# Feed-forward chunks with weights stationary, four-kilobyte expert loads, and rooms held later in a joined kernel

## The chip, the cores and the metric

The kernel runs on one core of one Trainium2 chip. The metric is the device time of one execution in microseconds (us). TensorE (PE) multiplies a stationary 128 x 128 block by moving columns into banks of PSUM; VectorE (DVE), ScalarE (ACT) and GpSimd (POOL) work on vectors; SyncE (SP) issues most DMA loads from HBM into SBUF. Each engine takes its own instructions in program order.

## What is computed

x has 256 tokens of 1024 features, everything in float32. Two layers of a first block are followed by two layers of a second block. Cut to what matters here:

```python
def swiglu(x, w_gate, w_up, w_down):
    return (silu(x @ w_gate) * (x @ w_up)) @ w_down

def first_block(x, ...):
    for l in range(2):
        x = x + 0.5 * swiglu(rms_norm(x, ffn1_norm[l]), ...)   # 1024 -> 2816 -> 1024
        h = rms_norm(x, mix_norm[l])
        ...                                                    # three attentions, gated and merged
        x = x + merged @ w_out[l]
        x = x + 0.5 * swiglu(rms_norm(x, ffn2_norm[l]), ...)

def second_block(x, mem, ...):
    for l in range(2):
        ...                                                    # linear attention and spatial gating
        x = layer_norm(DN_ALPHA * x + h, ...)
        h = mem_xattn(x, mem, wq[l], wk[l], wv[l], wo[l])      # keys: mem @ wk[l], 256 memory rows
        x = layer_norm(DN_ALPHA * x + h, ...)
        h = grouped_moe(x, ...)                                # 16 experts, 1024 -> 512 -> 1024, 2 per token
        x = layer_norm(DN_ALPHA * x + h, ...)
```

In `grouped_moe`, each expert computes `silu(x @ w_gate[e]) * (x @ w_up[e]) @ w_down[e]`, and its rows are added with the token's gate weight.

## The kernel before

**Stages.** TensorE goes through four feed-forward blocks (FFN) with the mixing stages between them, then for each layer of the second block: linear attention and gating, attention to the memory, sixteen experts. The keys of the memory for layer 1 are made right after the experts of layer 0, since the weights lie in the same stream.

**The weight stream.** All large weights come in units of 512 KB (128 partitions x 1024 floats) in the order of use. SBUF is cut into "rooms" of one unit. `load_ahead` (L262 to L274) puts the next unit into a free room; its DMA is issued by SP at L272. `take`/`hold` set rooms aside for other data, `give` returns them. Eight DMA semaphores go round over all DMA issues, so an issue waits until the eighth before it has landed, whichever engine issued that. PE, ACT, DVE and POOL take instructions in the order in which the program is written; `tick` lets queued side work (`spawn`, generators) go on between products.

**Products in float32.** `mm3` makes one product out of three fast ones: a weight is split into a rounded part (`whi`, ACT, L310) and its rest (`wlo`, DVE, L284), and so is the other factor. `pump` (L276) does the splitting ahead of use. Expert weights are marked `whole`: they are used unsplit with plain float32 products, and `pump` stops at any open whole unit when it runs ahead.

**FFN** (`gated`, L515 to L626). The 2816 hidden columns go in chunks, `CUTS` (L46): 512, 256 and four times 512. Of each chunk `into` makes the gate and then the up product, with x transposed (`xt`) stationary and the weights as moving columns, for two halves h of 128 tokens. ACT takes silu of the gate; DVE multiplies by the up product (L609). The result has tokens on its partitions and must be transposed before it can be the stationary factor of the down product: `turned` (L552) does up to four transposes (L558), an ACT copy (L561) and a DVE subtraction (L562). These stand after the second unit of the next chunk's gate. `down` adds to four banks `ys`. `last_down` ends each (half h, column half j), whose result DVE adds to x (L633), and transposes of the new x (L432) follow.

**Experts** (`moe`, L1700 to L2022). Each expert gets up to 64 token places. `gather(q)` collects the rows of x for four experts by products with a 0/1 matrix `pick` (L1834), the results copied by DVE (L1840) or ACT (L1842) into `xg`. `into(e)` (L1925) makes gate and up for the expert in one bank, in four steps u; `turn(e)` transposes (L1939), takes silu and multiplies (L1942); `down(e)` (L1950) makes the down product, scaled into two parts (L1956, L1957); `way_back(e)` makes the transposed 0/1 matrix and gate weights (L1851 on POOL, L1856, L1859, L1860); `scatter(e)` (L1966) adds the expert's rows to `ys`. The loop over e is at L1987 to L2018. In it `turn(e)` comes in step 0 of `into(e+1)` and `scatter(e-1)` in step 2; the gathers for experts 4 to 15 are spawned at e = 1, 4 and 8. Transposes and gathers share the banks "tp", products the banks "mm": three of "mm" and one of "tp" (L1975).

**Memory** (`memory`, L1341 to L1356, and `turned`, L1358 to L1377). In layer 0, `ME` = 9, 12, 20 sets the experts: from e = 9 eight rooms are set aside, at e = 12 the memory rows are loaded into `stage` (L1347, issued by ACT), and after 20 ticks they are transposed (L1354, copies at L440). `turned` multiplies the key weights, stationary, with the transposed memory of 256 columns (L1371 to L1373).

Of the kernel before, what the change touches and what calls it, by code (L numbers as in the profile page):

```python
# [42 lines left out]
ME = 9, 12, 20  # L43
P0 = (0,), (0,)
FN = 9, 9, 2, 4
CUTS = [512, 256, 512, 512, 512, 512]  # L46
# [23 lines left out]
def the_kernel(  # L70
# [90 lines left out]
    def columns(c0, n, pool, *loads):  # L161
# [5 lines left out]
        def put():  # L167
            pt = bank("mm")[:, :n]
            nc.tensor.transpose(pt, rows, ident[:n, :n])
            nc.vector.tensor_copy(col[:, c0:c0 + n], pt)  # L170
# [93 lines left out]
    def load_ahead(upto=None):  # L264
# [3 lines left out]
        while len(loads) < min(len(units), upto or len(units)) and free:  # L268
            at = free.pop(0)
            w, c0, n, k0, m, _, _ = units[len(loads)]  # L270
            r = block(at, [UNIT], name="raw")[:, :m * n].rearrange("p (k n) -> p k n", n=n)
            nc.sync.dma_start(r, w[k0 * P:(k0 + m) * P, c0:c0 + n].rearrange("(k p) n -> p k n", p=P))  # L272
# [3 lines left out]
    def pump(most=1, hurry=False, upto=None):  # L276
# [12 lines left out]
        while len(parts) < len(units) and (most > 0 if upto is None else len(parts) <= upto):  # L289
# [7 lines left out]
            if upto is None and any(whole is True for *_, whole in units[now["closed"]:len(parts)]):  # L297
                break
# [216 lines left out]
    def gated(xt, ready, chunks, scale, factor, last=True, renew=None, between={}, up="tp"):  # L515
# [3 lines left out]
        ys = []  # L519

        def into(tag, halves, hooks, done):
            W = Taken()
            o = [bank(tag)[:, :W.n] for _ in range(NH)]
            if halves == "start":

# [13 lines left out]
            order = [(h, u) for h in range(NH) for u in range(W.count)] if halves else \  # L539
                [(h, u) for u in range(W.count) for h in range(NH)]  # L540
            for i, (h, u) in enumerate(order):
                for k in W.ks(u):
                    mm3(o[h], *xt.at(h, k), *W(k), k == 0, k == KD - 1)
                if h:
                    W.close(1)
                if u == W.count - 1:
                    done(h, o[h])
                tick()
                for at, f in hooks:
                    if at == i + 1:  # L550
                        f()

        def turned(h, u, n):

            tp = tbank()
            nf = n // P
            for f in range(nf):
                nc.tensor.transpose(tp[:, f], u[:, f * P:(f + 1) * P], ident)  # L558
            uh = t2(FR).rearrange("p (f t) -> p f t", t=P)
            ul = t2(FR).rearrange("p (f t) -> p f t", t=P)  # L560
            nc.scalar.activation(uh[:, :nf], tp[:, :nf], AF.Copy)  # L561
            nc.vector.tensor_sub(ul[:, :nf], tp[:, :nf], uh[:, :nf].bitcast(FT))  # L562
            return uh, ul

        def down(c, ut):
            W = Taken()
            if not ys:
                ys.extend([bank(ACC[h]) for _ in range(2)] for h in range(NH))
            for f in range(W.kt):
                for h in range(NH):  # L570
                    for j in range(2):
                        mm3(ys[h][j], *(t[:, f] for t in ut[h]), *W(f, j), c == 0 and f == 0, False)
# [4 lines left out]
        def last_down(c, ut, gs):  # L577
            W = Taken()
            if not ys:
                ys.extend([bank(ACC[h]) for _ in range(2)] for h in range(NH))  # L580
            for h in range(NH):
                for j in range(2):
                    for f in range(W.kt):
                        mm3(ys[h][j], *(t[:, f] for t in ut[h]), *W(f, j), c == 0 and f == 0, last and f == W.kt - 1)
                        if (h, j) == (1, 1):
                            W.close(1)
                        if h == j == 0 and f == 1:
                            ut[1] = turned(1, late[1], late[2])
                        if f == W.kt - 1 and renew:
                            gs[h].append(spawn(renew(h, j, ys[h][j])))  # L590
                        if f % 2:
                            tick()
# [46 lines left out]
    def mixing_constants(fb, tmp):  # L639
# [52 lines left out]
        def distances():  # L692

            for put in puts:
                put()
# [1415 lines left out]
```

## Time and profile before

| | |
|---|---|
| three runs, median (lowest to highest) | 2193.13 us (2188.81 to 2196.97) |
| the profiled execution | 2191.49 us |
| its span in the profile | 2189.8 us |
| TensorE busy | 97% of the span, 11117 instructions |
| VectorE, ScalarE, GpSimd busy | 51%, 41%, 8% |
| moved by DMA | 490.48 MB, mean 224 GB/s |

The page of the profile gives the busy time of each engine over the whole span. A view of windows gives the same for stretches, with TensorE's granted clock (PEclk, 1.00 is full speed), the busy share of the DMA engines and the rate. A view of waits gives what an engine stood idle for. A timeline lists an engine's instructions in order, like neighbours put together.

### The profile page before, as it was taken

The numbers are of one execution on the slowest core, as the hardware profiler recorded it, in microseconds if no ns is written. First come the engines' busy times: TensorE is split into PE (matmuls) and PEld (weight loads), VectorE is DVE, ScalarE is ACT, GpSimd is POOL, SyncE is SP. The second block draws the span as 40 slices with busy tenths as digits, with TensorE's granted clock in tenths as the row PEclk, the third lists the DMA queues.
The fourth block names the chain that finished last, engine by engine and source line by source line (L and its number), as shares of the span: only waits on it lengthen the run. The fifth ranks groups of instructions, "written<-read, shape, count | busy, mean of one in ns | idle before, by whom it ended". The sixth has DMA issues, their size and how long they took to land. (4 is left out here: it accounts for less than half of the span.)

```text
span 2189.8 us, 29392 instructions
## 1 busy us (share of the span) xinstructions
PE 2117.0 (97%) x11117; PEld 1554.0 (71%) x11117; DVE 1118.9 (51%) x1999; ACT 892.4 (41%) x1424; POOL 172.5 (8%) x231
## 2 busy tenths in 40 slices
PE   8999999999999999999999999989999999989997
PEld 6778878788888888787888887963333677953332
DVE  6445787554555547866554547651111558341112
ACT  5444555454444446554544454521111454421111
POOL 1000100100000002102000002011000111010000
PEclk9999999999999999999999999999999999999999
DMA  7554643556556655535756555679998936589996
GB/s 250 187 181 149 211 145 111 178 177 200 174 172 193 196 159 171 187 98 173 242 183 190 158 170 198 207 258 338 393 394 297 360 116 236 178 313 383 394 393 247
DMA packets 240076, 490.48 MB, mean 224 GB/s; under 512 B 17539, under 2 KB 44851, under 8 KB 239923
## 3 DMA queue, kind: packets, MB, share of 16 engines
q1 hardware_dynamic: 239634, 487.42, 65.9%
q8 instruction: 92, 1.51, 0.3%
q10 hardware_dynamic: 288, 1.05, 0.1%
q14 instruction: 62, 0.50, 0.1%
HBM read 487.34 MB, written 1.07 MB: 223 GB/s over the span
## 5 line engine op out<-in xcount | busy, mean ns | idle before, releaser
L284 DVE TENSOR_TENSOR wlo<-raw,whi 128x1024 fp32r<-128x1024 f32 (+1 forms) x508 | 614.7, 1228 | 292.7 <-ACT whi L310 288.3
L310 ACT ACTIVATE whi<-raw 128x1024 fp32r<-128x1024 f32 (+1 forms) x508 | 525.1, 1052 | 293.3 <-PE tp L359 115.7
L1925 PE MATMUL mm<-raw,xg 128*64 128x512 f32 x1024 | 243.7, 604 | 7.7 <-PEq L1981 7.0
L357 PE MATMUL accB<-whi,xt 128*128 128x512 f32 (+3 forms) x448 | 176.2, 393 | 0.0
L359 PE MATMUL accB<-whi,xt 128*128 128x512 f32 (+3 forms) x448 | 165.5, 369 | 0.0
L358 PE MATMUL accB<-wlo,xt 128*128 128x512 f32 (+3 forms) x448 | 165.3, 369 | 0.0
L1925 PEld LDWEIGHTS mm<-raw,xg 128*64 128x64 f32 x1024 | 69.8, 137 | 133.5 <-issue 123.0
L357 PE MATMUL tp<-whi,xt 128*128 128x512 f32 (+1 forms) x384 | 143.8, 374 | 0.0
L359 PE MATMUL tp<-whi,xt 128*128 128x512 f32 (+1 forms) x384 | 143.4, 373 | 0.0
L358 PE MATMUL tp<-wlo,xt 128*128 128x512 f32 (+1 forms) x384 | 142.5, 371 | 0.0
L357 PE MATMUL mm<-whi,xt 128*128 128x512 f32 (+1 forms) x320 | 121.2, 379 | 1.4 <-DVE nbias L715 0.7
L359 PE MATMUL mm<-whi,xt 128*128 128x512 f32 (+1 forms) x320 | 118.3, 370 | 0.0
L358 PE MATMUL mm<-wlo,xt 128*128 128x512 f32 (+1 forms) x320 | 117.6, 368 | 0.0
L1950 PE MATMUL mm<-raw,t 128*64 128x512 f32 x512 | 117.3, 599 | 0.0
L1930 ACT ACTIVATE t<-mm 128x512 f32<-128x512 f32 x32 | 19.1, 597 | 188.4 <-PE mm L1925 188.4
L359 PEld LDWEIGHTS accB<-whi,xt 128*128 128x128 f32 x448 | 84.1, 188 | 15.1
L357 PEld LDWEIGHTS accB<-whi,xt 128*128 128x128 f32 x448 | 84.5, 189 | 13.3 <-issue 1.0
L358 PEld LDWEIGHTS accB<-wlo,xt 128*128 128x128 f32 x448 | 84.5, 189 | 11.6
L1859 DVE TENSOR_SCALAR back<-tp 128x256 fp32r<-128x256 f32 x32 | 13.6, 425 | 149.2 <-PE tp L1856 149.2
L609 DVE SCALAR_TENSOR_TENSOR t<-tp,ss,t 128x512 f32<-128x512 f32 (+1 forms) x48 | 33.8, 704 | 104.9 <-PE tp L359 104.9
L359 PEld LDWEIGHTS tp<-whi,xt 128*128 128x128 f32 x384 | 72.1, 188 | 13.5
L358 PEld LDWEIGHTS tp<-wlo,xt 128*128 128x128 f32 x384 | 72.1, 188 | 13.4
(515 smaller groups left out, 3950.2 us busy)
## 6 DMA issues: line engine op xcount, KB each, us to landing
raw<-in_w_gate_dram SPq DMA_DIRECT2D x128, 512.0 KB
raw<-in_w_up_dram SPq DMA_DIRECT2D x128, 512.0 KB
raw<-in_w_down_dram SPq DMA_DIRECT2D x128, 512.0 KB
raw<-in_w_in_dram SPq DMA_DIRECT2D x120, 512.0 KB
raw<-in_ffn_w_gate_dram SPq DMA_DIRECT2D x88, 512.0 KB
raw<-in_ffn_w_up_dram SPq DMA_DIRECT2D x88, 512.0 KB
raw<-in_ffn_w_down_dram SPq DMA_DIRECT2D x88, 512.0 KB
raw<-in_w_out_dram SPq DMA_DIRECT2D x32, 512.0 KB
```

What stands on the lines that cost most here:

```text
L284: eng.tensor_sub(lo, r, hi.bitcast(FT))
L310: nc.scalar.activation(hi, r, AF.Copy)
L357: nc.tensor.matmul(o, xh, wh, start=first, stop=False)
L358: nc.tensor.matmul(o, xh, wl, start=False, stop=False)
L359: nc.tensor.matmul(o, xl, wh, start=False, stop=last)
L609: nc.vector.scalar_tensor_tensor(ss[h], o, factor(h), ss[h], op0=OP.mult, op1=OP.mult)
L1859: nc.vector.tensor_scalar(bk, tp, 0.0, None, op0=OP.is_gt)
L1925: nc.tensor.matmul(p[half(i)], xgs[e // 4][k // 4][:, k % 4, e % 4], W.whole(k, i), start=k == 0, stop=k == KD - 1)
L1930: nc.scalar.activation(c[e], p, AF.Copy)
L1950: nc.tensor.matmul(p[half(j)], uu[e][:, f], W.whole(f)[:, j * 512:(j + 1) * 512], start=f == 0, stop=f == 3)
```

## The change

Four parts.

1. **FFN.** The first chunk stays at 512 columns; the other 2304 go in nine chunks of 256. For these, `into_turned` takes a 128 x 128 block of the weight as the stationary factor and the 256 tokens of `xt` as moving columns, so that the result lies transposed already. Its normalisation factor now lies along the free axis: at chunk 1 two small products and a copy make `roots`, and DVE multiplies the gate by it ahead of silu. Each product is split into its parts without a transpose; only the first chunk's goes through `turned`. The last chunk's up product is made one block of 128 after the other. `last_down` takes a new order. The side work in `between` moves behind the gate and from the "mm" to the "tp" banks, in one step more.
2. **Expert weights.** Gate and up units are loaded so that partition p holds adjacent rows: two rows, 4 KB, in one piece, where before it was pieces of 2 KB. The copies of x for the gathers are permuted to match (`eighths`).
3. **The order of the experts.** Two banks "mm" and two "tp". `turn(e)`, `way_back(e+1)`, `scatter(e-1)` and one quarter of the next gather all stand in step 1 of `into(e+1)`. POOL's part of the way back is issued ahead of `into`. The rooms of `xg` are taken at the start and kept until e = 15, and the memory attention sets aside 6 rooms instead of 4.
4. **Memory of layer 1.** `ME` = 12, 13, 14: the eight rooms are set aside from e = 12, the memory rows loaded at e = 13, and transposed after 14 ticks. `pump` may split later units while up to four whole units are open: the key weights while the last expert's down products run.

```diff
-ME = 9, 12, 20
+ME = 12, 13, 14
-CUTS = [512, 256, 512, 512, 512, 512]
+CUTS = [512] + 9 * [256]
@@ load_ahead
-            nc.sync.dma_start(r, w[k0 * P:(k0 + m) * P, c0:c0 + n].rearrange("(k p) n -> p k n", p=P))
+            if whole is True and m > 1:
+                nc.sync.dma_start(r, w[:, c0:c0 + n].rearrange("(p k) n -> p k n", p=P)[:, k0:k0 + m])
+            else:
+                nc.sync.dma_start(r, w[k0 * P:(k0 + m) * P, c0:c0 + n].rearrange("(k p) n -> p k n", p=P))
@@ pump
-            if upto is None and any(whole is True for *_, whole in units[now["closed"]:len(parts)]):
+            if upto is None and sum(whole is True for *_, whole in units[now["closed"]:len(parts)]) > 4:
                 break
@@ gated
+        ys = [[bank(ACC[h]) for _ in range(2)] for h in range(NH)]
...
+        def into_turned(tag, done, hook=None, in_turn=False):
+            W = Taken()
+            o = [bank(tag)[:, :S] for _ in range(2)]
+            for fs in ((0,), (1,)) if in_turn else ((0, 1),):
+                for u in range(W.count):
+                    for k in W.ks(u):
+                        xh, xl = xt.both(k)
+                        for f in fs:
+                            wh, wl = (t[:, f * P:(f + 1) * P] for t in W(k))
+                            mm3(o[f], wh, wl, xh, xl, k == 0, k == KD - 1)
+                            if k == KD - 1:
+                                done(f, o[f])
+                        if (k + 1) % (4 // len(fs)) == 0:
+                            tick()
+                    if 1 in fs:
+                        W.close(1)
+                    if hook and u == 0:
+                        hook()
+        def parts(u, to):
+            nc.scalar.activation(to[0], u, AF.Copy)
+            nc.vector.tensor_sub(to[1], u, to[0].bitcast(FT))
+            return to
...
+        def last_down(ut):
+            W = Taken()
+            gs = [[], []]
+            for i, (h, j, f) in enumerate(((0, 0, 0), (0, 1, 0), (1, 0, 0), (0, 0, 1), (0, 1, 1), (1, 0, 1), (1, 1, 0),
+                                           (1, 1, 1))):
+                mm3(ys[h][j], *at(ut, h, f), *W(f, j), False, f == 1)
+                if f:
+                    gs[h].append(spawn(renew(h, j, ys[h][j])))
+                if i % 2:
+                    tick()
+            W.close()
+            return gs
...
+            if c == 1:
+                p = bank("tp")[:, :S]
+                for h in range(NH):
+                    nc.tensor.matmul(p[:, h * P:(h + 1) * P], rs[h][:, 0:1].to_broadcast([P, P]), ident, start=True,
+                                     stop=True)
+                roots.append(pool.tile([P, S], FT, name="roots"))
+                nc.vector.tensor_copy(roots[0], p)
+            def silu_turned(f, o):
+                if f == 0:
+                    silus[0] = t2()
+                nc.vector.tensor_mul(silus[0][:, f * S:(f + 1) * S], o, roots[0])
+                if f:
+                    nc.scalar.activation(silus[0], silus[0], AF.Silu)
+            def product_turned(f, o):
+                v = silus[0][:, f * S:(f + 1) * S]
+                nc.vector.tensor_mul(v, o, v)
+                if f == 0:
+                    silus[1:] = [t2(FR), t2(FR)]
+                if c < chunks - 1 and f:
+                    parts(silus[0], silus[1:])
+                elif c == chunks - 1:
+                    parts(v, [t[:, f * S:(f + 1) * S] for t in silus[1:]])
...
+            into_turned("mm", silu_turned, hook)
             if c in between:
                 between[c]()
+            down(c - 1, (True, before) if c == 1 else ut)
+            into_turned("tp", product_turned, in_turn=c == chunks - 1)
+            ut = False, silus[1:]
@@ moe
-        xg_rooms, xn_rooms = [], take(4, 4)
+        xg_rooms, xn_rooms = take(2, 2), take(4, 4)
+            eighths = lambda t, j: t.rearrange("p (k m) -> p k m", k=KD)[:, :, j * 64:j * 64 + 64]
-                    nc.scalar.activation(xn[0][h][:, j * 512:(j + 1) * 512], x[h][j], AF.Copy)
+                    nc.scalar.activation(eighths(xn[0][h], j), x[h][j].rearrange("p (m k) -> p k m", k=KD), AF.Copy)
...
-            turns.enter_context(banks(mm=3, tp=1))
+            turns.enter_context(banks(mm=2, tp=2))
...
-                if e in (1, 4, 8):
-                    gs.append(spawn(gather(len(gs))))
+                if e in (3, 7):
+                    rest_of = gather(e // 4 + 2)
+                    next(rest_of)
...
-                wt = spawn(way_back(e + 1))
-                into(e + 1, {0: lambda: turn(e), 2: lambda: e and scatter(e - 1)})
-                finish(wt)
+                pk = gated_places(e + 1)
+                def between():
+                    turn(e)
+                    way_back(e + 1, pk)
+                    if e:
+                        scatter(e - 1)
+                    next(rest_of, None)
+                into(e + 1, {1: between})
                 down(e, (lambda: turn(15)) if e == 14 else None)
```

## Rows read from the trace of the kernel before

**Rows 1.** The page, busy time of each engine: us, share, instructions.

```profile
PE 2117.0 (97%) x11117; PEld 1554.0 (71%) x11117; DVE 1118.9 (51%) x1999; ACT 892.4 (41%) x1424; POOL 172.5 (8%) x231
```

**Rows 2.** Windows in one FFN: window, us, engines' busy us, PEclk, DMA, GB/s.

```profile
656.75:823.15 166.40, 166.00 (x802) 138.54 (x800) 84.26 (x93) 73.82 (x94) 0.79 (x2) 1.00 0.57 181
674.16:679.81 5.65, 5.65 (x49) 5.65 (x48) 1.21 (x2) 2.12 (x2) 0.00 (x0) 1.00 0.39 116
696.76:707.74 10.98, 10.98 (x49) 9.01 (x48) 3.62 (x4) 4.24 (x4) 0.00 (x0) 1.00 0.60 205
741.60:753.48 11.88, 11.88 (x58) 9.84 (x57) 7.28 (x8) 4.85 (x6) 0.00 (x0) 1.00 0.65 203
...
811.48:814.87 3.39, 2.99 (x16) 2.15 (x13) 2.77 (x4) 0.60 (x1) 0.00 (x0) 1.00 0.88 279
```

**Rows 3.** Windows in layer 0's experts: without a gather, with, and several.

```profile
1586.23:1599.08 12.85, 12.85 (x65) 4.48 (x63) 1.93 (x4) 1.67 (x3) 1.19 (x2) 1.00 1.04 395
1599.08:1618.37 19.29, 17.67 (x96) 8.39 (x94) 3.98 (x8) 2.86 (x5) 1.19 (x2) 1.00 1.04 392
1534.00:1645.00 111.00, 107.76 (x542) 42.29 (x542) 18.54 (x40) 15.06 (x27) 8.72 (x15) 1.00 1.04 394
```

**Rows 4.** Window at the end of layer 0's experts.

```profile
1645.75:1665.00 19.25, 19.25 (x96) 6.75 (x94) 3.11 (x6) 2.74 (x5) 1.21 (x3) 1.00 0.45 160
```

**Rows 5.** Timeline of PE, 1668 to 1684: start, us, instruction, idle before.

```profile
1670.11 3.65 PE L1950 MATMUL mm<-raw,t 128*64 128x512 f32 x16
1673.95 1.07 PE L1925 MATMUL mm<-raw,xg 128*64 128x512 f32 x2 [0.18 <-DMA raw<-in_w_gate_dram]
...
1677.16 0.66 PE L1939 MATMUL tp<-ident,t 128*128 128x128 f32 x4
```

**Rows 6.** Waits of PE, 1670 to 1730: us in total, times, longest.

```profile
PE mm L1373 <- DVE wlo L284: 4.6, 3, 2.6
PE tp L1856 <- DVE mem L440: 1.5, 1, 1.5
PE tp L1354 <- DVE mem L440: 1.4, 1, 1.4
PE tp L1354 <- DVE gw L1860: 0.9, 1, 0.9
```

**Rows 7.** Windows in the key products, weights stationary, 256 columns.

```profile
1251.40:1271.30 19.90, 19.90 (x178) 19.90 (x177) 11.73 (x12) 10.26 (x16) 0.00 (x0) 1.00 0.86 270
...
1737.50:1740.20 2.70, 2.70 (x25) 2.70 (x24) 2.44 (x4) 2.09 (x3) 0.00 (x0) 1.00 1.09 334
```

**Rows 8.** Waits of PE, 1477 to 1670.

```profile
PE tp L1834 <- DVE t L1942: 2.9, 3, 1.1
PE tp L1834 <- ACT xg L1842: 2.1, 3, 0.7
PE tp L1856 <- DVE t L1942: 1.1, 1, 1.1
```

**Rows 9.** Timeline of DVE, 198 to 205.

```profile
199.16 0.75 DVE L609 SCALAR_TENSOR_TENSOR t<-tp,ss,t 128x512 f32<-128x512 f32 x1 [0.31 <-PE tp L359]
...
201.61 0.69 DVE L562 TENSOR_TENSOR t<-tp,t 128x512 fp32r<-128x512 f32 x1 [0.56 <-ACT t L561]
```

**Rows 10.** Timeline of SP's queue, 1568 to 1584: issues of the loads.

```profile
1569.71 0.38 SPq L272 DMA_DIRECT2D raw<-in_w_up_dram  x1
1571.07 0.37 SPq L272 DMA_DIRECT2D raw<-in_w_gate_dram  x1
...
1574.98 0.38 SPq L272 DMA_DIRECT2D raw<-in_w_up_dram  x1
1576.26 0.37 SPq L272 DMA_DIRECT2D raw<-in_w_gate_dram  x1
```

**Rows 11.** Timeline of SP's queue, 2148 to 2176: the last weight loads.

```profile
2148.59 7.08 SPq L272 DMA_DIRECT2D raw<-in_w_down_dram  x6
```

**Rows 12.** Waits of SP's queue, 1640 to 1670.

```profile
SPq L272 <- DMA stage<-in_mem_dram: 19.5, 2, 19.2
```

More of the change, by code (lines that the diff above doesn't have):

```diff
@@ L512, in first_norm, with gated, into @@
         return xt, rs
-    def gated(xt, ready, chunks, scale, factor, last=True, renew=None, between={}, up="tp"):
-        ys = []
-        def into(tag, halves, hooks, done):
+    def gated(pool, xt, ready, chunks, rs, renew, between):
+        ys = [[bank(ACC[h]) for _ in range(2)] for h in range(NH)]
+        def into(tag, done, ordered):
             W = Taken()
             o = [bank(tag)[:, :W.n] for _ in range(NH)]
-            if halves == "start":
+            if ordered:
                 for i, parts in enumerate(((0, 0), (0, 1), (1, 0))):
@@ L538, in into @@
                 return
[L539 to L563, printed above, removed]
+            for u in range(W.count):
+                for h in range(NH):
+                    for k in W.ks(u):
+                        mm3(o[h], *xt.at(h, k), *W(k), k == 0, k == KD - 1)
+                    if h:
+                        W.close(1)
+                    if u == W.count - 1:
+                        done(h, o[h])
+                    tick()
@@ L571, in down @@
                     for j in range(2):
-                        mm3(ys[h][j], *(t[:, f] for t in ut[h]), *W(f, j), c == 0 and f == 0, False)
+                        mm3(ys[h][j], *at(ut, h, f), *W(f, j), c == 0 and f == 0, False)
                     if h:
@@ L575, in down @@
                     tick()
-        def last_down(c, ut, gs):
+        def last_down(ut):
             W = Taken()
[L579 to L592, printed above, removed]
@@ L692, in distances @@
         def distances():
-            for put in puts:
-                put()
-            pv = bank("mm")[:12, :384]
+            pv = bank("tp")[:12, :384]
             nc.tensor.matmul(pv, ct[:, 384:396], ct[:, :384], start=True, stop=True)
@@ L704, in distances, with positions @@
             nc.vector.tensor_scalar(nsink, nsink, -1.0, None, op0=OP.mult)
-            pp = bank("mm")
+        def positions():
+            for put in puts:
+                put()
+            pp = bank("tp")
             nc.tensor.transpose(pp[:, :32], pr, ident[:32, :32])
@@ L1852, in way_back @@
                                             gates[:, h, e:e + 1], None, op0=OP.mult)
-                yield from wait(WB)
+                return pk
+            def way_back(e, pk):
                 tp = tbank()[:, :2]
@@ L2064, in the_kernel @@
             memT = new_memory(4)
-            parts = memory(memT[0], "mm", 2)
+            parts = memory(memT[0], "tp", 2)
             step = lambda: next(parts, None)
```

103 lines of the change are left out of this document (49 added, 54 removed).

## The prediction

> **What bounds the kernel now.** I read the busy shares first: TensorE is busy for 97% of the span, every other engine for 51% or less [rows 1]. So time comes from three places only: columns that TensorE streams, the pitch at which it streams them, and its few waits. Then I took stretches. In a feed-forward block (FFN) TensorE works through 166.00 of 166.40 us at a granted clock of 1.00, which is the 2.4 GHz level, and DMA is at 0.57 [rows 2]: matmul work alone sets that time. In the expert stretches TensorE is almost as full, but DMA stands at 1.04 and 394 GB/s [rows 3]: the loads run slower than the products and live on a lead built up earlier. At the end of layer 0's experts that lead breaks: for 19.25 us the core moves only 160 GB/s [rows 4], and waits follow [rows 5, 6]. The waits views name who was late.
>
> **FFN, four of them.** Before, 48 matmuls of 512 columns take 10.98 us (228.8 ns each) and 48 of 256 columns 5.65 us (117.7 ns) [rows 2]. The gate and up products of the chunks after the first are 384 of the one and 96 of the other: 87.9 + 11.3 = 99.2 us per FFN. After, the same columns are 18 blocks of 128 x 8 x 2 x 3 = 864 matmuls of 256 columns with the weight stationary. The trace has that very form in the key products: 113 ns in the best stretch (19.90 us, 178 records, two of them not matmuls of this kind), and 25 in 2.70 us, with 119.9 ns between neighbours, in the worst [rows 7]. I take 116 ns, between them and near the FFN's own 117.7: 100.2 us, +1.0 (97.9 to 103.6). The weight loads of this form are as long as the stretch in the row, so the array has little slack behind them.
> Halving the moving columns is what the Trainium skill advises against ("TensorE: Matmul & The Clock Gate", sections Back-to-back issue gap and Why this matters for your kernels: 512 columns 518 cycles, 256 columns 262, keep dimensions at 512 or more). By its table two halves cost 1.2% more than a whole, some 1.1 us per FFN; the rows, 2 x 113.3 against 228.8 at best and 2 x 119.9 at worst, reach from a small gain to 5%. The row decides.
> The results now lie transposed, so 36 of 44 transposes per FFN go. Eight of them lengthen 48 matmuls from 10.98 to 11.88 us [rows 2], 0.9 per eight: -4.0. The transpose just ahead of the last down products makes that stretch 3.39 with 2.99 busy, where twelve matmuls want 2.75 [rows 2]: -0.65. Added are two small fp32 matmuls and a copy for the roots; I price them as one round trip through a bank, 0.9, like the mean of the three 2.9 us of waits for a bank in [rows 8], with 0.2 (the matmuls alone) as the low end. Added on DVE are two multiplications per gate block; DVE has 84.26 of 166.40 busy [rows 2] and I expect some 58%. The cover that decides: from a product to its two split parts the old kernel needs 199.16 to 202.30, 3.1 us, with another split between [rows 9]; the next chunk's gate, 48 x 0.116 = 5.6 us, runs meanwhile. Without that cover each chunk would cost the difference, 2 to 3 us. The last down product is put in a new order in which all four quarters finish in its last 3.5 us, so the next stage's renewal follows more tightly: I take +0.9 (0.3 to 2).
> Sum: +1.0 - 4.0 - 0.65 + 0.9 + 0.9 = **-1.9 per FFN, -8 for four** (by the pitch alone -17 to +6). Loads of the narrower chunks come in 1-KB rows, but DMA at 0.57 and 181 GB/s [rows 2] has room; nothing is late there.
>
> **Experts, both layers.** An expert without a gather takes 12.85 us, one with it 19.29 with 17.67 busy [rows 3]. The gathers, turns and way-backs share one transpose bank and wait on its readers: 2.9 + 2.1 + 1.1 = 6.1 us in layer 0 [rows 8], and the same three numbers in layer 1. With two banks, and one quarter of a gather per expert, each bank's reader has a turn of the other bank to finish: **-6.1**. The four hooks become one per expert, so TensorE changes less often between matmul kinds; no row prices a change alone, the excess of a gather expert over a plain one after waits and its 4 x 1.13 us of products is under 0.4 per gather, and I estimate **-1.5** (0 to -2). The product bank count falls from 3 to 2: a gate-up result is copied by ACT while the down product fills the other; the first gather alone uses these two and may wait 0 to 1 us. POOL's selection is issued one expert-part earlier; POOL is idle for 92% [rows 1]. Strided copies of x for the permuted rows: 0 to +3 per layer, taken at 0 since ACT and DVE are far from full. Layer 1: **-7.6** (-10 to -4).
> *Packets.* Gate and up weights go from 2-KB to 4-KB pieces, which down weights already have. SP issues a unit when the one eight before has landed; the pace is 1.36 us for units that follow gate and up loads and 1.28 for those that follow down loads [rows 10]. An expert's twelve units take 12 x 524.288 KB / 394 GB/s = 15.97 us [rows 3]; all at 1.28 it is 15.36. TensorE needs (16 x 12.85 + 3 x 6.44)/16 = 14.06 now and 13.58 after. So over 16 experts the loads lose 30.6 us now and 28.5 after: the lead, which has some 8 us over at the end of layer 1 (the last unit is issued by 2155.7 and lands about 10 later, the span having 24 left) [rows 11], holds.
> Two sections of the Trainium skill ("DMA: Bandwidth & Descriptors") pull against this term: Where 436 GB/s comes from sets about 358 GB/s as the HBM limit, by which packet size would change nothing, as in rival B below; the trace's 394 GB/s contradicts that. Why small descriptors are slow gives a fixed few cycles per descriptor, by which I estimate 2% rather than the rows' 5.5%; the row decides.
>
> **End of layer 0.** SP stands 19.2 us on the loads of the memory rows, which ACT issues only at its place in expert 12 [rows 12]; nothing is loaded meanwhile [rows 4]. Afterwards eight products take from 1673.95 to 1677.16, 3.21 us, where sixteen had just taken 3.65 [rows 5]: 1.4 lost, and with two like stretches beside it some 3.0 us. The memory transposes wait on the single bank 1.5 + 1.4 + 0.9 = 3.8 us, and the key products wait 4.6 us on split weights [rows 6]. After, the memory step is queued one expert later (what waits behind its two loads is again SP's whole weight queue, through the shared semaphores), two banks take the 3.8, the shorter stop and faster units the 3.0. The key weights come earlier by about 16 x 0.6 + 2 = 12 us while TensorE comes earlier by 14, so that the new right to split them under the last four down units gets something to split, but not everything: I take half of 4.6, 2.3 (0 to 4.6). Layer 0: -6.1 - 1.5 - 3.8 - 3.0 - 2.3 = **-16.7** (-22 to -8).
>
> **Sum.** -8 - 7.6 - 16.7 = -32.3 from the profiled execution's 2191.5 (span 2189.8): 2159.2. That execution lies 1.6 below the median 2193.1 of the runs shown, so 2161 as a median.
>
> **The rivals.**
> *E, better pitch:* all 864 matmuls at 113.3 ns: 864 x 2.7 ns x 4 = 9.3 less, **2152**. For it speaks the long key stretch, which had splits on ACT and DVE beside it [rows 7]; against it that the FFN's own 256-column products stay at 117.7 [rows 2].
> *C, worse pitch:* 119.9 ns: 864 x 3.9 ns x 4 = +13.5, **2174**. For it speaks that weight loads fill the whole stretch [rows 7], so each small hitch counts; the stretch of the worst row had DMA and splits beside it as an FFN has.
> *B, the loads don't quicken:* descriptors stay as short in effect, or reads of a 16-KB pitch lose what longer pieces gain. Then 38.2 us of lead are wanted where 38.6 are there, and the 3.0 and 2.3 at the end of layer 0 stay, for the early split has nothing to split: +5.3, **2166**; two waits at the layers' ends could make it 2172.
> *D, slower than before:* each partition now owns eight adjacent weight rows (16 KB), and a gate or up unit reads two of them, so its 4-KB pieces lie 16 KB apart. If that slows a unit beyond 1.36 us, each further 0.1 us costs 12.8 us per layer. At 330 GB/s, 1.59 us, an expert loads in 17.84; (17.84 - 13.58) x 16 - 38.6 = 29.6 per layer, **2220**. Down loads, whole rows in order, say nothing of it; no row here reads at that pitch in that order. [...]
>
> **How the numbers follow.** Forecast A 0.45, E 0.15, B 0.15, C 0.17, D 0.08. The range takes in E, B and C with a margin of their unknown ends (roots, renewal, strided copies): 2146 to 2184; outside are D and about 0.1 of tails. About 0.5%, 11 us, is what a measurement here can tell from no change. Faster: 0.42 of A, E, 0.11 of B, 0.10 of C, 0.78 in all; the same 0.03 + 0.04 + 0.07 = 0.14; slower 0.08.
>
> **What would show it.** Right: FFN of 164 to 165 us with 256-column pitches near 116 ns; no transposes but eight in an FFN's middle; no tp wait in the expert stretches; SP's pace 1.28 throughout; no DMA wait in experts 13 to 15; split of key weights seen before the last down product ends. Wrong: an FFN over 170 us or waits of its down products on split parts (the chain is longer than 5.6 us); a gate unit above 1.36 us; TensorE waiting on raw weights in the middle of a layer.

## The result

The changed kernel takes 2156.1 us (2154.5 to 2156.4) where the kernel before, run beside it, takes 2191.0: a ratio of 0.9835 (0.9813 to 0.9858), some 35 us less. Forecast were 2161 and a range of 2146 to 2184. The profiled execution spans 2154.7 us, 35.1 less than that of before. Where the 35.1 us lie, by the starts of stages in the two traces (first product of the stage on TensorE; one execution each; differences taken before rounding):

| stage | before | after | difference | forecast |
|---|---|---|---|---|
| start to the memory keys of layer 0 (four FFNs, mixing) | 1249.2 | 1236.6 | -12.6 | -8 |
| keys, gating, memory attention of layer 0 | 228.4 | 227.5 | -0.9 | 0 |
| experts of layer 0 | 238.1 | 230.0 | -8.0 | -14.4 |
| keys, gating, memory attention of layer 1 | 235.4 | 232.6 | -2.8 | -2.3 |
| experts of layer 1 to the end | 238.8 | 228.0 | -10.8 | -7.6 |

So the sum came out within 3 us of the forecast's 32.3, but out of other terms.

The page of the kernel after, busy time of each engine; TensorE is as full as in [rows 1], with 1408 more matmuls:

```profile
PE 2089.4 (97%) x12525; PEld 1611.4 (75%) x12525; DVE 1147.0 (53%) x2107; ACT 884.1 (41%) x1420; POOL 170.9 (8%) x231
```

Windows of the kernel after (window, us, busy us of PE, PEld, DVE, ACT, POOL, granted clock, DMA share, GB/s): an FFN from the end of its first chunk to the next stage's first product, the same up to its last down product, then a stretch of the next stage; experts of layers 0 and 1, and one expert without a gather:

```profile
650.46:814.85 164.39, 162.41 (x1157) 150.99 (x1156) 93.61 (x120) 71.58 (x94) 3.28 (x12) 1.00 0.61 190
650.46:810.85 160.39, 160.39 (x1146) 149.44 (x1145) 90.43 (x111) 68.15 (x82) 3.28 (x12) 1.00 0.61 191
...
814.85:817.46 2.61, 2.61 (x8) 2.09 (x7) 1.75 (x9) 2.61 (x10) 0.55 (x1) 0.52 0.00 0
1500.00:1600.00 100.00, 100.00 (x517) 41.40 (x514) 17.72 (x37) 14.16 (x25) 8.31 (x14) 1.00 1.03 409
1990.00:2120.00 130.00, 130.00 (x670) 53.17 (x668) 21.82 (x46) 18.49 (x33) 10.69 (x18) 1.00 1.03 409
2101.21:2113.60 12.39, 12.39 (x64) 4.67 (x62) 1.84 (x4) 1.67 (x3) 1.19 (x2) 1.00 1.02 407
1684.90:1691.74 6.84, 0.04 (x2) 0.00 (x0) 3.33 (x4) 3.80 (x5) 0.00 (x0) 0.71 1.04 384
1691.74:1698.06 6.32, 6.32 (x27) 5.08 (x28) 6.25 (x10) 1.95 (x2) 0.46 (x1) 0.51 1.09 369
```

The first row answers to the 166.40 us of [rows 2]: 164.39. The fourth and fifth answer to [rows 3]: 409 GB/s instead of 394, and TensorE busy without a gap. The sixth answers to the 12.85 us. The last two are new: 6.84 us in which TensorE does nothing, and 6.32 us at half its clock after that.

Waits of TensorE in the kernel after, layer 0's experts and keys (us in total, times, longest):

```profile
PE accA L2005 <- ACT t L1995: 6.8, 1, 6.8
PE mm L1964 <- PEq L2020: 3.7, 1, 3.7
PE mm L1989 <- DMA raw<-in_w_down_dram: 1.0, 2, 0.8
PE tp L1871 <- DVE t L1981: 0.8, 1, 0.8
PE mm L1964 <- DMA raw<-in_w_up_dram: 0.6, 1, 0.6
PE mm L1964 <- DMA raw<-in_w_gate_dram: 0.3, 1, 0.3
```

Of the 6.1 us of bank waits in [rows 8], 0.8 is left. Of [rows 6] nothing is left: neither the 3.8 us of the memory transposes nor the 4.6 us on split key weights. In their place stands one wait of 6.8 us: the last expert's scatter waits for its own scaled copy (L1995 is L1956 of before).

### The profile page after: what moved, and what is told of

The parts are those of the page before. It is cut to its first block, busy times and chain, and to the rows that moved or that the text cites. A ratio compares the mean times of both kernels' runs of the same rounds, so it can differ in the third digit from the quotient of the medians.

```text
span 2154.7 us, 32302 instructions
## 1 busy us (share of the span) xinstructions
PE 2089.4 (97%) x12525; PEld 1611.4 (75%) x12525; DVE 1147.0 (53%) x2107; ACT 884.1 (41%) x1420; POOL 170.9 (8%) x231
## 5 line engine op out<-in xcount | busy, mean ns | idle before, releaser
L361 PE MATMUL mm<-xt,whi 128*128 128x256 f32 x576 | 159.7, 277 | 0.0
L361 PE MATMUL tp<-xt,whi 128*128 128x256 f32 x576 | 159.4, 277 | 0.0
L362 PE MATMUL tp<-xt,whi 128*128 128x256 f32 x576 | 159.3, 277 | 0.0
L363 PE MATMUL tp<-xt,wlo 128*128 128x256 f32 x576 | 159.2, 276 | 0.0
L363 PE MATMUL mm<-xt,wlo 128*128 128x256 f32 x576 | 159.1, 276 | 0.0
L362 PE MATMUL mm<-xt,whi 128*128 128x256 f32 x576 | 159.0, 276 | 0.0
L1996 DVE SCALAR_TENSOR_TENSOR t<-mm,gw,t 128x512 fp32r<-128x512 f32 x32 | 24.0, 751 | 225.5 <-ACT t L1995 225.5
L644 DVE TENSOR_TENSOR t<-tp,t 128x256 f32<-128x256 f32 x72 | 27.9, 424 | 181.2 <-PE tp L363 181.2
L362 PEld LDWEIGHTS tp<-xt,whi 128*128 128x128 f32 x576 | 108.3, 188 | 1.5
L361 PEld LDWEIGHTS tp<-xt,whi 128*128 128x128 f32 x576 | 108.1, 188 | 1.5
L363 PEld LDWEIGHTS tp<-xt,wlo 128*128 128x128 f32 x576 | 108.2, 188 | 0.0
L362 PEld LDWEIGHTS mm<-xt,whi 128*128 128x128 f32 x576 | 108.2, 188 | 0.0
L361 PEld LDWEIGHTS mm<-xt,whi 128*128 128x128 f32 x576 | 108.1, 188 | 0.0
L363 PEld LDWEIGHTS mm<-xt,wlo 128*128 128x128 f32 x576 | 108.1, 188 | 0.0
```

The source lines that it names most:

```text
L361: nc.tensor.matmul(o, xh, wh, start=first, stop=False)
L362: nc.tensor.matmul(o, xh, wl, start=False, stop=False)
L363: nc.tensor.matmul(o, xl, wh, start=False, stop=last)
L644: nc.vector.tensor_mul(v, o, v)
L1996: nc.vector.scalar_tensor_tensor(yl, p, gw, yh.bitcast(FT), op0=OP.mult, op1=OP.subtract)
```

## The experiments

Times are medians beside the kernel before on the same chip. Where a few us matter I also compare, from the traces, the stretch from the first gate-up product of layer 0's experts to that of layer 1's: 473.4 us before, 462.6 after. The changed kernel's second trace (e13, below) takes 460.0 there, so 2 or 3 us in one trace of this stretch tell nothing by themselves. "Seam" is the time from an FFN's last down product to the next stage's first product.

### The first part alone

The kernel before with the diff's changes in `CUTS`, `gated`, `ffn`, the side steps and their banks; the rest as before.

> The kernel before with the FFN part of the change alone. Theory from the two traces: each FFN's products come out cheaper by 5 to 7 us (113.8 ns per 256 columns, 36 transposes fewer) and 2 to 4.6 us of that are given back at the seam to the next stage, where transposes wait for split parts of the new x: 12 us faster than before, 2178 to 2180. Rival (the rest of the kernel paid for the four stages between, or the seam eats more): at most 6 us faster.

2179.6 us, ratio 0.9951 (0.9938 to 0.9965), 10.4 us less: the theory's size within 2 us. The products are cheaper than forecast. In the kernel after, on TensorE:

```profile
652.28 0.28 PE L361 MATMUL mm<-xt,whi 128*128 128x256 f32 x1
652.39 0.28 PE L362 MATMUL mm<-xt,whi 128*128 128x256 f32 x1
652.50 0.28 PE L363 MATMUL mm<-xt,wlo 128*128 128x256 f32 x1
652.62 0.28 PE L361 MATMUL mm<-xt,whi 128*128 128x256 f32 x1
```

Three products in 0.34 us: 113 ns each, the best pitch of [rows 7]; the mean over all 864 of an FFN is 113.8. But the seam gives part of it back:

```profile
810.61 0.40 PE L363 MATMUL accB<-whi,t 128*128 128x512 f32 x1
810.85 0.60 PE L436 MATMUL tp<-ident,x 128*128 128x128 f32 x4
813.05 0.66 PE L436 MATMUL tp<-ident,x 128*128 128x128 f32 x4 [1.60 <-DVE xt L449]
814.08 1.12 PE L436 MATMUL tp<-ident,x 128*128 128x128 f32 x4 [0.38 <-DVE xt L449]
814.85 0.78 PE L361 MATMUL accA<-whi,xt 128*128 128x512 f32 x1
815.43 0.63 PE L362 MATMUL accA<-wlo,xt 128*128 128x512 f32 x1
```

The last down product ends the stretch at 810.85; the next stage's first product starts at 814.85, and its neighbours stand 0.42 to 0.58 us apart where 0.23 is usual. Up to 810.85 the FFN is 6.0 us shorter than the 166.4 of before; 4.0 go at the seam.

This FFN is the third of the four, and it gains least. The other three between the same two points, first before, then after:

```profile
37.46:212.35 174.89, 173.25 (x817) 140.98 (x816) 89.10 (x104) 73.80 (x94) 0.87 (x2) 1.00 0.58 181
467.25:633.78 166.53, 166.15 (x802) 138.64 (x800) 84.27 (x93) 74.47 (x95) 0.55 (x1) 1.00 0.58 183
1079.58:1249.22 169.64, 169.15 (x817) 139.95 (x816) 85.50 (x88) 73.46 (x85) 0.00 (x0) 1.00 0.59 188
```

```profile
37.75:208.14 170.39, 168.43 (x1171) 153.04 (x1170) 98.03 (x131) 71.87 (x93) 3.29 (x12) 1.00 0.62 194
464.70:628.38 163.68, 161.71 (x1155) 150.27 (x1154) 93.23 (x120) 71.20 (x92) 0.00 (x0) 1.00 0.60 192
1072.51:1236.60 164.09, 162.84 (x1167) 151.61 (x1166) 95.09 (x118) 70.19 (x83) 0.00 (x0) 1.00 0.63 201
```

The four gain 4.5, 2.9, 2.0 and 5.5 us, 14.9 in all. In the first and the last, side work runs between the products; why these two gain more is not worked out. The two mixing stages behind the first and the third give back 1.7 and 1.2 us: TensorE's waits in them are the same before and after, but its clock fell once more in each. With 0.9 us gained in the first chunk of the third FFN, and a start 0.3 us later, that is the -12.6 of the table.

### The seam's order

```diff
-    def finish(*gs):
+    def finish(*gs, own=False):
         while any(g in active or any(g is q for _, q in queue) for g in gs):
-            tick(split=0)
+            if own and any(g in active for g in gs):
+                for g in gs:
+                    if g in active and next(g, active) is active:
+                        active.remove(g)
+            else:
+                tick(split=0)
...
-                finish(*halves[h])
+                finish(*halves[h], own=True)
```

and the same in `into` of the first chunk.

> The changed kernel; where a stage begins with the products of token half 0, only the renewal of half 0 is finished ahead of them, and the transposes of half 1 are left to come between those products (in the changed kernel all four transposes stand ahead of the first product). Theory (the seam after an FFN is a matter of order: TensorE waits for the bank of the third and fourth transpose, 2 us, and its clock falls to 1.2 GHz for the next 2.5 us): the waits on split parts of the new x fall from 7.1 us in all to under 2, the clock stays up: 4 to 10 us faster than the changed kernel, 2146 to 2152. Rival (the chain of update, transpose, copy and subtraction of half 0 sets the seam, and the transposes of half 1 hide in it): within 2 us of 2156.

2148.9 us, ratio 0.9814 (0.9793 to 0.9835). The seam of the same FFN:

```profile
809.32 0.60 PE L441 MATMUL tp<-ident,x 128*128 128x128 f32 x4
811.53 0.66 PE L441 MATMUL tp<-ident,x 128*128 128x128 f32 x4 [1.60 <-DVE xt L454]
811.94 0.48 PE L366 MATMUL accA<-whi,xt 128*128 128x512 f32 x1
```

The first product follows 2.62 us after the down products instead of 4.00, and the clock stays up. But the wait of 1.60 us stays too: the third transpose needs a bank that DVE empties, and DVE has four updates, the last two of them below, and then the first four of eight subtractions to do before:

```profile
809.04 1.40 DVE L672 SCALAR_TENSOR_TENSOR x<-accB,ss,x 128x512 f32<-128x512 f32 x2
810.35 2.15 DVE L454 SCALAR_TENSOR_TENSOR xt<-tp,col,xt 128x128 fp32r<-128x128 f32 x8
```

So the waits on split parts of the new x, 7.1 us in the changed kernel's trace, fall to 6.1 and not to under 2; that step of the theory fails. Nor is the clock the order's doing: e7 below, without this edit, has the changed kernel's waits at this seam (1.60 and 0.38 us), its first product follows after 3.65 us, and its clock is 1.00 there:

```profile
812.76 0.66 PE L436 MATMUL tp<-ident,x 128*128 128x128 f32 x4 [1.60 <-DVE xt L449]
813.80 0.66 PE L436 MATMUL tp<-ident,x 128*128 128x128 f32 x4 [0.38 <-DVE xt L449]
814.21 0.48 PE L361 MATMUL accA<-whi,xt 128*128 128x512 f32 x1
```

So the order is worth some 1.0 us at this seam (3.65 to 2.62), and as much at the first two (3.63 to 2.62 at both); the fourth stays at 2.2. Over the whole stretch from the first FFN to the keys this kernel takes 1225.0 us, the changed kernel 1228.1 and e7 1224.4, and the ratio's interval overlaps the changed kernel's: the time shows neither the theory's 4 to 10 us nor the rival; only e11 and e12, below, bear on it again.

### Shorter pieces again

```diff
-            if whole is True and m > 1:
+            if False:
```

with `xn` in plain order.

> The changed kernel with gate and up units of the experts in pieces of 2 KB again, and the copies of x unpermuted; all else as changed. Theory (longer pieces quicken the stream, and layer 0's end lives on it): the pace of SP's issues goes from 1.28 back to 1.36 us for gate and up units, the stream from 409 to 394 GB/s, the loads at the end of layer 0 come some 8 to 10 us later and TensorE waits that long for raw and key weights; in layer 1 the lead covers it, or a few us show: 6 to 14 us slower than the changed kernel, 2162 to 2170. Rival (packets give nothing in time, the loads are hidden): within 2 us of 2156.

2166.0 us, ratio 0.9892 (0.9875 to 0.9908), 10 us more than the changed kernel. The same window of layer 1, and waits late in it:

```profile
1990.00:2120.00 130.00, 130.00 (x668) 53.10 (x666) 21.03 (x44) 18.49 (x33) 10.68 (x18) 1.00 1.04 393
```

```profile
2128.63 1.04 PE L1964 MATMUL mm<-raw,xg 128*64 128x512 f32 x2 [0.36 <-DMA raw<-in_w_gate_dram]
2129.91 2.42 PE L1964 MATMUL mm<-raw,xg 128*64 128x512 f32 x8 [0.23 <-DMA raw<-in_w_up_dram]
2132.61 1.93 PE L1964 MATMUL mm<-raw,xg 128*64 128x512 f32 x6 [0.29 <-DMA raw<-in_w_up_dram]
2134.47 0.66 PE L1978 MATMUL tp<-ident,t 128*128 128x128 f32 x4
```

The rate falls from 409 to 393 GB/s and the lead runs out in layer 1's last two experts: sixteen products from 2128.63 to 2134.47 take 5.84 us where they take 3.5 in the changed kernel. The theory placed the loss in layer 0; the traces put 5.8 us in layer 1's experts (233.8 against 228.0) and 2.4 in the stretch of layer 0. The other 2.1 us lie ahead of the experts, which start at 1466.2 for 1464.1; the changed kernel's own second trace has 1466.4, so they need not be the pieces' doing.

### Three steps instead of one hook

```diff
-                into(e + 1, {1: between})
+                into(e + 1, {0: lambda: turn(e), 1: lambda: (way_back(e + 1, pk), next(rest_of, None)),
+                             2: lambda: e and scatter(e - 1)})
```

> The changed kernel, with the one hook in step 1 of the gate-up products spread over three steps: turn in step 0, way back and gather quarter in step 1, scatter in step 2. Banks, packets and all else as changed. Theory (an expert without a gather fell from 12.85 to 12.4 us because TensorE changes less often between kinds of products): such an expert goes back to 12.7 to 12.9 us; layer 1 is 5 to 8 us longer, layer 0 less, since loads set the time at its end: 6 to 12 us slower than the changed kernel. Rival (two transpose banks, which stay, made it): an expert stays at 12.4 to 12.5, within 2 us of the changed kernel.

2162.0 us, ratio 0.9875 (0.9860 to 0.9891), 6 us more than the changed kernel run beside it (2155.8). An expert without a gather:

```profile
2083.27:2096.10 12.83, 12.83 (x65) 4.48 (x63) 1.93 (x4) 1.67 (x3) 1.19 (x2) 1.00 1.02 407
```

12.83 instead of 12.39, as before the change, with two banks for transposes and the longer pieces in place. In the timelines the 32 gate and up products take 1.82 + 1.87 + 1.87 + 1.76 = 7.32 us in four pieces and 3.53 + 3.49 = 7.02 in two, the turn 0.58 against 0.49 and the way back 0.37 against 0.32: 0.44 us. So the mechanism holds for such an expert, and the rival falls. But ten of the sixteen experts have a gather quarter with them, and these differ by only 0.25 us (13.78 against 13.53): layer 1 takes 231.3 us against 228.0, 3.3 more and not 5 to 8. Layer 0 takes 230.4 against 230.0, with a first expert at full clock where the changed kernel's loses 2.6 us at half clock. The profiled execution of e10 was its fastest, so the 6 us of the medians cannot be placed stage by stage.

### The fourth part undone, and its halves

The split rule alone:

```diff
-            if upto is None and sum(whole is True for *_, whole in units[now["closed"]:len(parts)]) > 4:
+            if upto is None and any(whole is True for *_, whole in units[now["closed"]:len(parts)]):
```

> The changed kernel with one line put back: splitting stops again at any open expert unit, so no key weight is split before the last down product is issued. Theory (early split blocks ACT): in the changed kernel four rounded copies stand on ACT ahead of the last expert's scaled copy and wait for key weights that have not landed; the scatter products wait 6.8 us for that copy and TensorE's clock falls to 1.2 GHz for some 4 us behind it. Without the early split the wait falls under 0.5 us, the clock stays at 1.00, and 3 to 5 us of waits on split key weights come back in the key products: 2 to 7 us faster than the changed kernel, 2152 +- 3. Rival (the loads set the time): the key weights land when they land, the 6.8 us only move to the key products: within 1.5 us of the changed kernel, 2156.

2153.4 us, ratio 0.9831 (0.9816 to 0.9847): the same time as the changed kernel within the intervals. The waits moved, as the rival said:

```profile
PE mm L1410 <- DVE wlo L288: 4.6, 3, 2.6
PE mm L1408 <- ACT whi L314: 1.0, 1, 1.0
```

What the early split does is seen on ACT in the changed kernel:

```profile
1683.45 1.06 ACT L314 ACTIVATE whi<-raw 128x1024 fp32r<-128x1024 f32 x1 [2.54 <-DMA raw<-in_wk_x_dram]
1687.35 1.06 ACT L314 ACTIVATE whi<-raw 128x1024 fp32r<-128x1024 f32 x1 [2.84 <-DMA raw<-in_wk_x_dram]
1688.62 1.06 ACT L314 ACTIVATE whi<-raw 128x1024 fp32r<-128x1024 f32 x1 [0.21 <-DMA raw<-in_wk_x_dram]
1690.06 1.06 ACT L314 ACTIVATE whi<-raw 128x1024 fp32r<-128x1024 f32 x1 [0.38 <-DMA raw<-in_wk_x_dram]
1691.02 0.67 ACT L1995 ACTIVATE t<-mm,gw 128x512 fp32r<-128x512 f32 x1
```

Four rounded copies wait for loads, and the last expert's scaled copy, whose product was done at about 1683.4, stands behind them until 1691.02. The mechanism is as the theory has it; that removing it is a gain is not shown, for the key products then wait on weights split late (e1's stretch is 461.1 us against 462.6 and 460.0).

The rule and the old `ME` = 9, 12, 20 together:

> The changed kernel with its fourth part undone: rooms set aside from expert 9, memory rows loaded at expert 12, 20 ticks, and splitting stops at any open expert unit. Theory (the fourth part is worth little: its later stop of SP saves what its early split spends): the stop of SP is again some 15 to 19 us and comes one expert earlier, key products wait 4 to 6 us on split weights, raw weights 1 to 3 us: 2 to 6 us slower than the changed kernel, 2156 to 2162. Rival (the fourth part carries the gain at the end of layer 0): 8 us or more slower, 2164 and up. Second rival: the same or faster, 2156 or less.

2156.1 us, ratio 0.9851 (0.9830 to 0.9871), stretch 460.1 us: the second rival. These times show no gain from the fourth part.

### The memory rows on SP's queue

```diff
-                    mt = spawn(memory(memT[0], "tp", 2, ME[2], apart=True))
+                    mt = spawn(memory(memT[0], "tp", 2, ME[2], apart=False))
```

> The changed kernel, but the memory rows of layer 1 are loaded by SP's queue instead of ACT's. Theory (ACT's place in program order holds the loads up): SP stands 12.2 us in the changed kernel because the eighth issue before is a load that ACT reaches only in expert 13; on SP's own queue that stop goes, later units are issued about 10 us earlier, the 1.9 us of waits on raw weights in experts 14 and 15 and most of the 6.8 us wait of the last scatter go, and the clock does not fall: 6 to 11 us faster than the changed kernel, 2147 +- 3. Rival (rooms hold the loads up): the stage rooms come free no earlier, SP stands as long on them, with every later weight behind: within 2 us of 2156, or some us slower.

2160.9 us, ratio 0.9865 (0.9847 to 0.9883), stretch 468.0, 5.4 to 8.0 us longer; the medians say 4 to 5 us slower. SP's stop is gone, but the rows come late. TensorE's waits and SP's issues:

```profile
PE tp L1391 <- DMA stage<-in_mem_dram: 14.7, 1, 14.7
```

```profile
1655.61 9.28 SPq L276 DMA_DIRECT2D raw<-in_w_down_dram  x8
1665.84 0.38 SPq L276 DMA_DIRECT2D raw<-in_wk_x_dram  x1
1667.09 1.65 SPq L1384 DMA_DIRECT2D stage<-in_mem_dram  x2
```

Neither theory nor rival had this: SP works through the loads programmed ahead of the rows and reaches them at 1667.09, when TensorE already stands for them. So the load has to be written earlier: `ME` = 10, 11, 42.

> The changed kernel with the memory rows on SP's queue, as in e2, but put two experts earlier: rooms set aside from expert 10, rows loaded at expert 11, transposed after 42 ticks (so in expert 14 as before). Theory (in e2 the rows were late only because SP works through the loads ahead of them): rows land by about 1655, the 14.7 us wait of e2 goes, SP doesn't stop, key weights are issued 7 us earlier than in the changed kernel, the last scatter doesn't wait: 7 to 11 us faster than the changed kernel, 2145 to 2149. Rival (six rooms fewer ahead for two more experts let the raw weights run late): waits on raw weights in experts 12 to 15 of 5 us or more, no faster than 2153.

2151.6 us, ratio 0.9830 (0.9810 to 0.9849), stretch 455.5, 7.1 and 4.4 less than the changed kernel's two; of either, some 2.6 lie in the first expert, which both traces of the changed kernel spend in part at half the clock (10.9 and 11.0 us against 8.4). The interval overlaps the changed kernel's. Rows in SP's stream and no stop:

```profile
1632.15 0.33 SPq L274 DMA_DIRECT2D raw<-in_w_gate_dram  x1
1633.39 1.61 SPq L1384 DMA_DIRECT2D stage<-in_mem_dram  x2
```

Raw weights are waited for nowhere, but the last scatter still waits 7.0 us: the key weights are issued 10 us earlier, and TensorE arrives 9.6 us earlier too. With the late split on top:

> As e7, with splitting stopped again at any open expert unit. Theory (early split pays only where the key weights have landed): with the weights there in time the early split saves the 4.6 us of waits on split weights, so this run is 2 to 5 us slower than e7. Rival (the split is bound by ACT and DVE, not by landing): within 1 us of e7.

2148.3 us, ratio 0.9801 (0.9777 to 0.9825), stretch 456.4, within 1 us of e7 in the stretch: the rival. The key products wait `L1410 <- DVE wlo` 4.6 us in three waits, 2.6 the longest: the very numbers of [rows 6] and of e1, with key weights issued at quite other times. DVE ahead of the longest of the three:

```profile
1688.01 0.75 DVE L1332 SCALAR_TENSOR_TENSOR x<-x,bmv,rows 128x512 f32<-128x512 f32 x1
1688.68 1.22 DVE L288 TENSOR_TENSOR wlo<-raw,whi 128x1024 fp32r<-128x1024 f32 x1
```

So two of the waits, 3.8 of the 4.6 us, are set by DVE's queue, where the norm's statistics and updates stand ahead of the splits. Landing has a part in the first alone, 0.8 us: there ACT's rounded copy waited 2.3 us for its load. Last, e7 with nothing split until the scaled copy is issued:

```diff
-                    tick()
+                    tick(split=int(e < 14 or e + f == 18))
```

> As e7 (memory rows on SP's queue from expert 11), and in the last expert's down product nothing is split until its scaled copy is issued; then key weights are split at once, ahead of the norm's work on DVE. Theory (order on ACT, not early splitting as such, makes the 7 us wait): the last scatter waits under 0.5 us, the clock stays up, and the key products wait 1 to 3 us on split weights instead of 4.6 to 5.2: from the start of layer 0's experts to that of layer 1's 450 to 453 us, where e7 took 455.6, e8 456.4 and the changed kernel 462.6. Rival (landing of the key weights sets the time): waits on split weights of 5 us or more, 455 to 457 us.

2146.4 us, ratio 0.9804 (0.9784 to 0.9824), stretch 453.5. The scatter waits 0.3 us, but the 4.5 us on split weights stay, as in the rival. Only two splits come ahead of the norm's work on DVE, so the order that the theory wanted there was not reached. How the gain over the changed kernel divides between the rows' new place (2151.6), the late split (2148.3) and the copy's order (2146.4) is not shown, since these three intervals overlap.

### Together

> The changed kernel itself, as the yardstick for the runs beside it: 2153 to 2158.

2155.8 us, ratio 0.9846 (0.9829 to 0.9862).

> e11 and e9 together: memory rows early on SP's queue, scaled copy ahead of splits, and each half's renewal finished by itself at the start of a stage. If the gains add, 2 to 4 us less than e11 and 8 to 13 us less than the changed kernel run beside it; if the end of layer 0 eats what the seams give (loads set the time there), within 1 us of e11.

2142.5 us, ratio 0.9788 (0.9775 to 0.9802): 13 us less than the changed kernel beside it, 48 less than the kernel before. Its gain over e11, 3.9 us, is of the size foreseen, though the two intervals overlap; in the traces 2.6 of it lie ahead of the keys (1231.7 for 1234.3), where three seams take 2.6 us each instead of 3.6 and the clock fell once in both; the stretch behind takes 454.4 for 453.5. This version is faster than both kernels.

## Why the prediction was right, and where its steps were not

**The sum.** It came out 2.8 us from the forecast by errors that offset each other: the stages ahead of layer 0's experts, and layer 1's experts, gave 8.7 us more than forecast, layer 0's experts and the keys behind them 5.9 less. That so near a total came of it is partly luck.

**FFN pitch.** Taken at 116 ns, measured 113.8: rival E was the true case here. The term of +1.0 per FFN was -0.9. Rival E's total (2152) lies 4.1 us from the result and the forecast's 2161 lies 4.9 from it, so the total could not tell the two pitches apart; the trace does. Nothing of rival C is seen. The Trainium skill's table ("TensorE: Matmul & The Clock Gate", section Back-to-back issue gap) makes two halves cost 1.2% more than a whole by its cycles; here they cost 2 x 113.8 = 227.6 ns against the 228.8 of [rows 2], so the trace does not agree.

**Transposes and roots.** -4.0 and +0.9. Up to the last down product the FFN is 6.0 us shorter, near the -5.6 that -0.9, -4.0 and -0.65 let one expect. The roots' products cost 0.37 together with their neighbours; +0.9 was too much. Two transposes of the new x, 0.36 us each, moved behind that point into the seam. Of the 0.65 that I put down to the FFN's last transpose, 0.40 was something else: the wait of the new x's first transpose for DVE's update (L633, at 814.87 before). No down product waits on split parts, so the cover of 5.6 us held.

**Seam.** This is the mis-sized term: +0.9 (0.3 to 2) where 3.6, 3.6, 4.0 and 2.2 us pass at the four seams, and behind the third 2.6 us follow at a granted clock of 0.52 in the changed kernel's trace. I had counted the chain of one quarter; what counts is that four quarters go through DVE and two banks at once, with all transposes ahead of the first product. In the third FFN the sum (164.39 against 166.40, -2.0, forecast -1.9) came out by two errors of opposite sign. Over all four it did not: -14.9 where -8 was forecast, of which the falls of the clock in the mixing stages take some back. e4 shows -10.4 in all.

**Experts.** The bank waits fell from 6.1 to 0.8 us per layer: -5.3 for -6.1. Layer 1 came out at -10.8 for -7.6, so some 5.5 us are left for the change of kinds of products, forecast at -1.5 per layer (at most -2). Of these 3.3 are what e10 loses again in layer 1. The other 2 are not shown by a run of their own; they fit the gathers, whose quarters cost 1.1 us each beyond waits before and 0.95 in e10, where a quarter shares the way back's stop. I had bounded this term by the gather experts' excess rather than by comparing sixteen products in one piece and in two.

**Pieces.** 409 GB/s and 1.28 us per unit came as forecast (from 1.36 us that is 6%, not the 5.5% that I wrote); a pitch of 16 KB shows no cost, so rival D is out. Layer 1 has no wait on raw weights, neither before nor after. The Trainium skill's limit of about 358 GB/s for one core ("DMA: Bandwidth & Descriptors", section Where 436 GB/s comes from) disagrees with 409 GB/s on this core, and the same page's fixed cost per descriptor (section Why small descriptors are slow (HBM only)), 2% by my estimate, is under the 4% from 393 to 409.
e3 is rival B made real: 2166 forecast for it, 2166.0 measured, though the loss sits in layer 1 rather than at layer 0's end, so that agreement is partly chance.

**End of layer 0.** -16.7 was forecast and -10.8 came (-8.0 and -2.8). The 3.8 us of bank waits went as said; late raw weights still cost 1.9 us, though no DMA wait in experts 13 to 15 was to be a sign of being right. SP's stop on the memory rows is 9.5 us instead of 19.2. The step that failed is the early split: I took it to have something to split and to save 2.3 us. It did find work, but ACT takes instructions in order, and its waiting copies held the last scatter for 6.8 us; the clock then stayed at about half for 6.3 us, some 3 us of work. e1, e5 and e8 show that it saves about what it costs. I had named what stood behind SP's wait and not what stood behind ACT's.

**The clock in this comparison.** The way from start to keys differs by up to 5 us between executions of kernels that are the same there: 1233.1 in e10, where the clock fell once, 1238.5 in e13, where it fell four times. Counted as in the last section, these falls cost 1.7 and 6.8 us, which leaves 1231.4 and 1231.7. By the same count the changed kernel's first trace has 1231.5 left and the kernel before 1247.5; e4 has 1231.7. At equal clock the first part gains some 16 us up to the keys, where the profiled pair shows 12.6 and 8 was forecast. What stays open is why the clock fell more often in the changed kernel's two traces than in those of e7 and e10.

## What to carry to other kernels

Before letting an engine work ahead, list what stands behind that work in its queue: a copy that waits for a load holds up the next copy that another engine needs. When several results finish together instead of one after the other, price the seam by everything that passes through the shared engine and banks, not by one result's chain. A DMA belongs on the queue whose order suits it and must be written as many units ahead as that queue has in hand.

## What the runs showed of the hardware

After idle stretches TensorE came back at half its clock for a while, but not always. At the FFN's seam above it was granted 0.52 for 2.61 us after waits of 1.60 and 0.38 us; after the same two waits at the same seam (1.58 and 0.38 us in e10) e7 was granted 1.00, and e10 too. After 6.84 idle us at the end of layer 0 it was granted 0.51 for 6.32 us. Adding up (1 - granted clock) x 10 us over those windows of 10 us that lie below 0.99, without the last 20 us of the span, the kernel before loses 5.1 us of full-speed time, the changed kernel 15.3, e10 6.9 and e12 5.1. Some of that falls into waits themselves: counting only time in which TensorE was busy, it is 4.2, 12.4, 6.1 and 5.0. So some 8 us of the changed kernel's profile, beyond what the kernel before loses in this way, went not into waiting but into what followed the waits.

Stopping a run of products for another kind of product costs TensorE time of itself: 0.44 us per expert for two more stops (12.83 against 12.39, e10), with no wait recorded; 0.25 where a gather quarter goes along (13.78 against 13.53).
